# A retention and sparse-attention decoder: layer 1's y transposed by VectorE and carried through memory for three heads of four, and compression blocks made three ahead

## The chip, the cores and the metric

The program runs on one core of a Trainium2 chip. Its metric is the device time of one execution in microseconds. Five engines work side by side, each through its own queue in order: TensorE (PE, with its weight loads listed apart as PEld), VectorE (DVE), ScalarE (ACT), GpSimd (POOL) and SyncE (SP), which here only issues DMAs. The kernel before took 1155.59 us (median of three runs, 1155.13 to 1158.02).

## The reference, cut to what matters

Two layers over 512 tokens of width 1024, all float32. Layer 1 is a retention layer of four heads; for each head (256 wide in q and k, 512 in v):

```
q, k = rotary(x_norm @ Wq), rotary(x_norm @ Wk) / 16
o    = ((q k^T) * decay) @ v
o    = (o - mean(o)) * rsqrt(var(o) + eps)          # over the head's 512 columns
y    = silu(x_norm @ Wg) * o                        # 512 tokens x 512, per head
h   += (y * gain) @ Wout[512 h : 512 h + 512]       # 1024 columns
```

Between the layers, K and V of the sparse attention are projected once, and two of them are compressed: every block of 32 tokens (stride 16, 31 blocks, four groups) gets a position term, is flattened to 4096 numbers and goes through a small network:

```
blocks = (sub-blocks + pe).reshape(4, 31, 32 * 128)
k_cmp  = gelu(blocks @ w1) @ w2                      # w1: 4096 x 256; the same for v_cmp
```

Layer 2 is sparse attention over these, with a gate, an output projection and a per-layer embedding; the change does not touch it.

## The kernel before, in words

Every product of two float32 matrices is made of three matmuls (`mm3`, L349): each operand is held as a rounded high part and a low part, and high x high, high x low and low x high are summed in PSUM. ScalarE makes a high part (a copy that rounds), VectorE the low part (a subtraction of the high part).

Weights come as a stream of 176 blocks of 512 KB in the order in which they are used (`order`, L48; class `Stream`, L118). A block lands in one of four raw buffers (`load`, L143, on SP), is multiplied by its gain on POOL where it has one and is narrow (`mul`, L176), gets its high part from ScalarE (`high`, L190 or L194) and its low part from VectorE (`low`, L205 or L209), in one of six slots. After each `low` the next load goes into the raw buffer that came free. `W.tick()` does one `low`, one `high` and one `mul` of the blocks that are next; where a tick stands in the program decides where these stand in the engines' queues. The order of the program's lines is the order in each queue: there is no scheduler.

Layer 1 goes head by head (L546 to L582). For heads 1 to 3 it makes four projections of 128 columns (`proj_rot`, L409: q twice, k twice), each 24 matmuls of 512 columns, each followed by two multiplications by cosine and sine on VectorE (`rot_mul`, L423) and a tick; `rot_split` (L426) finishes the rotation on POOL and splits it on ScalarE and VectorE. Among these stands the transposition of the previous head's y: `retention_yT` (L516) for each of four token tiles, four 128 x 128 transposes on TensorE (L519) into PSUM and a split from there (L364, L365) into yH and yL. Then `out_proj` (L535) multiplies the previous head's y by its 512 rows of the output weights: eight tiles of 12 matmuls, each reading all four 128-column pieces of yH and yL of one token tile. The last head's y is transposed later, at L656, and keeps TensorE in both kernels.

The compression (`compress`, L779) runs twice, for K and for V, as eight steps of 12 matmuls of 256 columns (o at L797). Step s needs the block s: an addition on POOL (L787) into one of two buffers, a high part on ScalarE (L789), and a low part on VectorE (L792), in one of four pairs. Before the first step blocks 0 and 1 are made; step s then makes block s + 2. The second compression is spread among the four query projections of group 0 (`q_proj`, L732) at L867 to L877: two steps after each of the first three, and one on either side of the second half of the fourth. The first key projection (`k_proj`, L758) follows.

Of the kernel before, what the change touches and what calls it, by code (L numbers as in the profile page):

```python
# [11 lines left out]
F32 = mybir.dt.float32  # L12
F32R = mybir.dt.float32r
BF = mybir.dt.bfloat16
AF = mybir.ActivationFunctionType
# [3 lines left out]
NT, NK = 4, 8  # L19
# [217 lines left out]
def decoder(ctx: ExitStack, tc: tile.TileContext, x, xT, stream, cst, msk, gains, fnorm, out):  # L237
    nc = tc.nc
    pe, act, dve, pool = nc.tensor, nc.scalar, nc.vector, nc.gpsimd
    ctx.enter_context(tc.manual_schedule())  # L240
    sb = ctx.enter_context(tc.tile_pool(name="sb", bufs=1))
    ps = ctx.enter_context(tc.tile_pool(name="ps", bufs=1, space=bass.MemoryType.PSUM))
    nF = 4096 + 1024 * RAWS + 700 + 8192
    nR = 8192 + 2048 * SLOTS + 15104
# [4 lines left out]
    def V(o, n):  # L249
        assert o + n <= nF, (o, n)  # L250
        return arenaF[:, o:o + n]

    def R(o, n):
        assert o + n <= nR, (o, n)
        return arenaR[:, o:o + n]
# [8 lines left out]
    fb = 4096 + 1024 * RAWS  # L264
# [7 lines left out]
    def psum(tag, shape=None):  # L272
        n = {"d": 2, "s": 3, "pt": 2, "o": 1}[tag]
        return ps.tile([128, 512], F32, name=tag, bufs=n)
# [34 lines left out]
    yH = R(rb + 10752, 2048).rearrange("p (c n) -> p c n", c=4)  # L309
    yL = R(rb + 12800, 2048).rearrange("p (c n) -> p c n", c=4)  # L310
    gate = V(fb, 2048).rearrange("p (t n) -> p t n", t=NT)
# [2 lines left out]
    cs = V(fb + 4096, 1024).rearrange("p (a n) -> p a n", a=2)  # L314
    dec = V(fb + 5120, 1024).rearrange("p (h n) -> p h n", h=2)
    yb = [V(fb + 6144 + 512 * i, 512) for i in range(2)]
    rx = V(fb, 4096).rearrange("p (k t n) -> p k t n", k=NK, t=NT)


# [5 lines left out]
    o = psum("o")  # L325
    for i in range(30):
        pe.matmul(o[:, :256], masks[:, :128], masks[:, :256], start=True, stop=True)
    for k in range(NK):
        nc.sync.dma_start(rx[:, k], xT[k // 2, :, 512 * (k % 2):512 * (k % 2) + 512])
        if k in (0, 2):  # L330
            c = slice(256 * k, 256 * k + 512)
# [26 lines left out]
    def wst(p, o, k0=0, k1=NK):  # L358

        mm3(o, [(p.h[:, k], p.l[:, k], aH[:, :, k], aL[:, :, k]) for k in range(k0, k1)],  # L360
            k0 == 0, k1 == NK)
# [47 lines left out]
    def proj_rot(h, b, c):  # L409
        p = W.get("rin", 0, 1024, b + 256 * h + 128 * c, 128)  # L410
        o = psum("s" if h == 0 and b else "d")
        wst(p, o, 0, 4)
        if h or c == 0:
            W.tick()
        wst(p, o, 4, 8)
        p.done()
        if h == 0:
            return o
        rot_mul(o, c)

    def rot_mul(o, c):
        for i in range(2):
            dve.tensor_mul(rot[:, 2 * c + i], o, cs[:, i])  # L423
        W.tick()

    def rot_split(H, L):  # L426
        pool.tensor_sub(rot[:, 0], rot[:, 0], rot[:, 3])
        pool.tensor_add(rot[:, 1], rot[:, 1], rot[:, 2])
        for i in range(2):
            c = slice(512 * i, 512 * i + 512)  # L430
            act.activation(H[:, c], rot[:, i], AF.Copy)
            dve.tensor_sub(L[:, c], rot[:, i], H[:, c].bitcast(F32))
# [41 lines left out]
    def run(g):  # L474
        for _ in g:
            pass
# [39 lines left out]
    def retention_yT(t, bank="pt"):  # L516
        p = psum(bank)
        for c in range(4):
            pe.transpose(p[:, 128 * c:128 * c + 128], gate[:, t, 128 * c:128 * c + 128], ident)  # L519
        p3 = p.rearrange("p (c n) -> p c n", c=4)  # L520
        c = slice(128 * t, 128 * t + 128)
        split_psum(yH[:, :, c], yL[:, :, c], p3)

    def out_tile(t, c, p, YH, YL):
        o = psum("s" if t % 2 else "d")
        for a in range(2):
            mm3(o, [(YH[:, 2 * a + k, 128 * t:128 * t + 128], YL[:, 2 * a + k, 128 * t:128 * t + 128],
                     p[a].h[:, k], p[a].l[:, k]) for k in range(2)], a == 0, a == 1)
        d = hacc[:, t, 512 * c:512 * c + 512]
        dve.tensor_add(d, d, o)  # L530
# [15 lines left out]
    for h in range(HEADS):  # L546
        if h == 0:
            p = [W.get("rin", 0, 1024, 128 * c, 128) for c in (0, 1)]
            o = [psum("d") for c in (0, 1)]
            for k in range(NK):  # L550
                for c in (0, 1):
                    wst(p[c], o[c], k, k + 1)
                if k % 4 == 3:
                    W.tick()
            for c in (0, 1):
                p[c].done()
            dve.tensor_copy(masks, yb[0][:, :M_END])
            o += [proj_rot(h, 1024, c) for c in (0, 1)]
            rotary_scale()
            for b in range(2):  # L560
                for c in range(2):
                    rot_mul(o[2 * b + c], c)
                rot_split(*((kH, kL) if b else (qH, qL)))
        else:
            proj_rot(h, 0, 0)
            retention_yT(0)
            retention_yT(1)
            proj_rot(h, 0, 1)
            rot_split(qH, qL)
            retention_yT(2)  # L570
            retention_yT(3)
            proj_rot(h, 1024, 0)
            proj_rot(h, 1024, 1)
            rot_split(kH, kL)
            run(out_proj("rout", h - 1, yH, yL))
        tokens("rin", h, 2048, v_evac, ("o", "s", "pt", "pt") if h == 0 else ("d", "d", "s", "s"))
        retention_scores(h)
        if h < 3:
            load_decay(h + 1)
        tokens("rin", h, 4096, g_evac, ("d", "d", "pt", "pt"))  # L580
        for t in range(NT):
            retention_out(t)  # L582
# [74 lines left out]
    p = [out_pieces("rout", 3, c) for c in range(2)]  # L657
# [121 lines left out]
    def compress(b):  # L779

        def block(s):
            B = blk[s % 2].rearrange("p (l g n) -> p l g n", l=4, g=4)
            src = ckv[:, b]
            src = bass.AP(tensor=src.tensor, offset=src.offset + 4 * s,
                          ap=[list(src.ap[0]), [1, 4], [512, 4], [16, 31]])
            pos = gn[:, (G_PEV if b else G_PEK) + 4 * s:][:, :4]
            pool.tensor_add(B[:, :, :, :31], src,  # L787
                            pos[:, :, None, None].to_broadcast([128, 4, 4, 31]))
            act.activation(bkH[s % 4], blk[s % 2], AF.Copy)  # L789
            if s > 1:  # L790
                W.tick()
            dve.tensor_sub(bkL[s % 4], blk[s % 2], bkH[s % 4].bitcast(F32))  # L792

        block(0)
        block(1)
        yield
        o = psum("o")[:, :256]  # L797
        for s in range(8):
            p = W.get("wv" if b else "wk", 512 * s, 512, 0, 256)
            H, L = bkH[s % 4], bkL[s % 4]  # L800
            mm3(o, [(H[:, 128 * l:128 * l + 128], L[:, 128 * l:128 * l + 128], p.h[:, l], p.l[:, l])
                    for l in range(4)], s == 0, s == 7)
            if s < 6:
                block(s + 2)
            if s == 7:
                act.activation(hid, o, AF.Gelu_apprx_tanh)
            if s > 5:
                W.tick()
            p.done()
            yield  # L810
        tp = psum("pt")[:, :256]
        for c in range(2):
            pe.transpose(tp[:, 128 * c:128 * c + 128], hid[:, 128 * c:128 * c + 128], ident)
        if b == 0:
            split_psum(hidH.rearrange("p c n -> p (c n)"), hidL.rearrange("p c n -> p (c n)"), tp)
        else:
            src = tp.rearrange("p (a n) -> p a n", n=32)[:, :, None, :].to_broadcast([128, 8, 4, 32])
            split_psum(hrH.rearrange("p a (r n) -> p a r n", r=4),
                       hrL.rearrange("p a (r n) -> p a r n", r=4), src)
        yield  # L820
        w2 = [w[:, 2 * b:2 * b + 2] for w in (w2p.h, w2p.l)]
        if b == 0:
            o = psum("s")[:, :128]
            mm3(o, [(w2[0][:, c], w2[1][:, c], hidH[:, c], hidL[:, c]) for c in range(2)], True, True)
            split_psum(kcH, kcL, o)
        else:
            o = psum("s")
            for g in range(4):
                mm3(o[:, 128 * g:128 * g + 128],
                    [(hrH[:, 4 * c + g], hrL[:, 4 * c + g], w2[0][:, c], w2[1][:, c])  # L830
                     for c in range(2)], True, True)
            act.activation(vcat[:96], o[:96], AF.Copy)
            dve.tensor_sub(vcat[32:64], o[32:64], vcat[32:64].bitcast(F32))
        yield
# [6 lines left out]
    p = v_pieces(0)  # L841
    W.tick(1)
    o = [psum(bank)[:, :304] for bank in ("d", "o", "d", "s")]
# [190 lines left out]
    for g in range(GROUPS):  # L1034
        f = fillers(g)
        for u in range(8):
            h = u // 2
# [4 lines left out]
            n = PLAN[u] if g == 3 else left - first if u % 2 else first  # L1042
# [37 lines left out]
        if g < 3:  # L1080
            p = v_pieces(g + 1)
# [4 lines left out]
    p = [W.get("nout", 1792, 256, 512 * c, 512) for c in (0, 1)]  # L1086
# [98 lines left out]
```

## Time and profile before

| | |
|---|---|
| median of three runs | 1155.59 us |
| profiled execution: its own time | 1155.31 us |
| its span in the trace | 1153.3 us |
| TensorE busy | 1132.1 us, 98% |
| VectorE, ScalarE, GpSimd busy | 710.4, 486.7, 317.4 us |
| mean granted TensorE clock | 0.997 of full |
| moved by DMA | 101.9 MB, mean 88 GB/s |

The trace is one execution. A line of it names the line of the kernel, the engine, the operation, the tiles it writes and reads, and a count. A time in brackets in the timeline is how long the engine was idle before, and what ended that. Ends of matmuls are modelled: a matmul of 512 columns is listed at 0.39 us, while the next one starts 0.23 us after it. Nearly all tiles are parts of two large ones, arenaF (float32) and arenaR (the split parts), so the line tells more than the name.

### The profile page before, as it was taken

What the parts mean: (1) busy time and instruction counts of PE and PEld (TensorE: products, weight loads), DVE (VectorE), ACT (ScalarE), POOL (GpSimd) and SP (SyncE); (2) the same over time, 40 slices, a digit from 0 to 9 for tenths busy, and PEclk for the clock granted to TensorE, in tenths of its full rate; (3) what the DMA queues carried; (4) which work ended last, traced back from release to release, by engine and by line L of the source; (5) the groups of instructions that cost most, each with busy time, mean ns of one, the idle gap of its engine ahead of it and who ended that gap; (6) DMA issues with size and microseconds to landing.
All of it is one profiled execution on the core that took longest, in us unless ns stands there. A gap on an engine that the chain in (4) does not pass through costs nothing. (4 is left out here: it accounts for less than half of the span.)

```text
span 1153.3 us, 15259 instructions
## 1 busy us (share of the span) xinstructions
PE 1132.1 (98%) x5812; PEld 964.3 (84%) x5812; DVE 710.4 (62%) x1226; ACT 486.7 (42%) x916; POOL 317.4 (28%) x357
## 2 busy tenths in 40 slices
PE   9999999999999999999899999999999999999997
PEld 7888888888888888988777889888898888988886
DVE  4746435544634665656577865778468774788555
ACT  6433223223323454545455433444345443444653
POOL 0212003002200212346645332354153431421012
PEclk9999999999999999999999999999999999999999
DMA  8422331222232123244531211222031211221211
GB/s 329 149 97 73 110 101 55 92 101 74 86 116 73 55 78 106 73 152 160 163 110 56 74 37 39 78 85 66 27 93 55 74 56 44 85 85 44 74 37 73
DMA packets 29593, 101.90 MB, mean 88 GB/s; under 512 B 3536, under 2 KB 3792, under 8 KB 29520
## 3 DMA queue, kind: packets, MB, share of 16 engines
q1 hardware_dynamic: 29088, 100.15, 26.8%
q8 instruction: 45, 0.74, 0.3%
q10 hardware_dynamic: 432, 0.79, 0.2%
q14 instruction: 28, 0.23, 0.1%
HBM read 98.83 MB, written 2.10 MB: 88 GB/s over the span
## 5 line engine op out<-in xcount | busy, mean ns | idle before, releaser
L355 PE MATMUL d<-arenaR 128*128 128x512 f32 (+2 forms) x2904 | 676.5, 386 | 2.4 <-ACT arenaR L136 1.0
L355 PEld LDWEIGHTS d<-arenaR 128*128 128x128 f32 x2904 | 524.5, 188 | 103.2 <-DVE arenaF L753 1.4
L355 PE MATMUL s<-arenaR 128*128 128x512 f32 (+8 forms) x1182 | 239.8, 354 | 0.7 <-ACT arenaR L364 0.5
L205 DVE TENSOR_TENSOR arenaR<-arenaF,arenaR 128x1024 fp32r<-128x1024 f32 (+1 forms) x142 | 191.7, 1369 | 70.5 <-ACT arenaR L190 70.3
L355 PEld LDWEIGHTS s<-arenaR 128*128 128x128 f32 x1182 | 200.3, 188 | 30.6 <-ACT arenaR L364 0.7
L190 ACT ACTIVATE arenaR<-arenaF 128x1024 fp32r<-128x1024 f32 (+1 forms) x142 | 145.8, 1048 | 105.6 <-PE s L355 68.4
L176 POOL TENSOR_TENSOR arenaF<-arenaF 128x512 f32<-128x512 f32 x108 | 135.3, 1276 | 99.2 <-DMA arenaF<-stream_dram 94.7
L355 PE MATMUL o<-arenaR 128*128 128x512 f32 (+3 forms) x744 | 128.8, 322 | 6.3 <-DVE arenaR L792 4.1
L967 POOL TENSOR_SCALAR arenaF<-arenaF 128x512 f32<-128x512 f32 (+3 forms) x128 | 67.2, 545 | 232.3 <-ACT arenaR L364 118.8
L355 PEld LDWEIGHTS o<-arenaR 128*128 128x128 f32 x744 | 114.3, 189 | 19.6 <-DVE arenaR L792 5.1
L954 ACT ACTIVATE arenaF<-s,arenaF 128x512 f32<-128x512 f32 (+3 forms) x128 | 67.1, 526 | 101.4 <-DVE arenaF L947 90.6
L365 DVE TENSOR_TENSOR arenaR<-pt,arenaR 128x512 fp32r<-128x512 f32 (+1 forms) x141 | 82.9, 618 | 36.9 <-ACT arenaR L364 34.3
L364 ACT ACTIVATE arenaR<-pt 128x512 fp32r<-128x512 f32 (+1 forms) x141 | 70.8, 541 | 73.3 <-PE pt L976 35.2
L371 POOL TENSOR_TENSOR arenaF<-arenaF 128x1 f32<-128x1 f32 (+1 forms) x25 | 14.2, 570 | 295.3 <-DVE arenaF L370 295.3
L355 PE MATMUL pt<-arenaR 128*128 128x512 f32 (+1 forms) x384 | 75.9, 349 | 0.0
L355 PEld LDWEIGHTS pt<-arenaR 128*128 128x128 f32 x384 | 62.7, 188 | 9.4
L209 DVE SCALAR_TENSOR_TENSOR arenaR<-arenaF,arenaR 128x512 fp32r<-128x512 f32 x64 | 45.7, 763 | 35.1 <-PE pt L355 21.4
L194 ACT ACTIVATE arenaR<-arenaF 128x512 fp32r<-128x512 f32 x64 | 43.1, 720 | 46.7 <-issue 22.3
L947 DVE TENSOR_REDUCE arenaF<-s 128x1 f32<-128x512 f32 (+3 forms) x128 | 59.9, 489 | 3.3
L1015 DVE TENSOR_TENSOR arenaF<-arenaF,d 128x512 f32<-128x512 f32 x64 | 42.4, 683 | 8.6 <-PE d L355 7.8
L976 PEld LDWEIGHTS pt<-arenaF 128*128 128x128 f32 x318 | 38.3, 141 | 10.7 <-DVE arenaR L365 3.1
L976 PE MATMUL pt<-arenaF 128*128 128x128 f32 x318 | 45.1, 273 | 1.9 <-DVE arenaR L365 1.9
(126 smaller groups left out, 704.8 us busy)
## 6 DMA issues: line engine op xcount, KB each, us to landing
arenaF<-stream_dram SPq DMA_DIRECT2D x174, 512.0 KB, 3.6
arenaF<-xT_dram SPq DMA_DIRECT2D x8, 256.0 KB, 5.3
arenaF<-x_dram SPq DMA_DIRECT2D x4, 512.0 KB, 8.4
out_dram<-arenaF SPq DMA_DIRECT2D x3, 512.0 KB, 2.6
arenaF<-cst_dram SPq DMA_DIRECT2D x4, 256.0 KB, 3.9
arenaF<-stream_dram ACTq DMA_DIRECT2D x2, 256.0 KB, 4.2
arenaF<-stream_dram SPq DMA_DIRECT2D x2, 256.0 KB, 5.9
arenaF<-cst_dram SPq DMA_DIRECT2D x1, 512.0 KB, 9.5
```

The lines of the kernel that those rows point to most:

```text
L176: self.nc.gpsimd.tensor_mul(r3[:, k], r3[:, k], g[:, k, None].to_broadcast([128, m // 2, w]))
L190: self.nc.scalar.activation(hi[:, :m * w], raw, AF.Copy)
L194: self.nc.scalar.activation(hi[:, c], raw[:, c], AF.Copy, scale=g[:, k:k + 1])
L205: self.nc.vector.tensor_sub(lo[:, :m * w], raw, hi[:, :m * w])
L209: self.nc.vector.scalar_tensor_tensor(lo[:, c], raw[:, c], g[:, k:k + 1], hi[:, c], op0=OP.mult, op1=OP.subtract)
L355: pe.matmul(o, a, b, start=start and i == 0, stop=stop and i == n - 1)
L364: act.activation(h, src, AF.Copy)
L365: dve.tensor_sub(l, src, h.bitcast(F32))
L947: dve.reduce_max(mx[:, i:i + 1], o[:, f:f + 128 * i + 128], axis=mybir.AxisListType.X, negate=True)
L954: act.activation(Pu[:, PO[i]:PO[i] + n], o[:, f:f + n], AF.Exp, bias=mx[:, i:i + 1], accum_out=sm_[:, i:i + 1])
L967: pool.tensor_scalar(w, w, sm_[:, i:i + 1], 1.0, op0=OP.mult, op1=OP.mult)
L976: pe.transpose(p[:, f:f + 128], Pu[:, PO[i] + 128 * j:PO[i] + 128 * j + 128], ident)
```

## The change

For heads 1 to 3 TensorE no longer transposes the previous head's y. VectorE transposes each 32 x 32 block of it in place (`retention_blocks`: two instructions for two token tiles, into a free stretch of arenaF, yt). Four DMAs write yt to a buffer in device memory, one for each of its four groups of 32 partitions, so that the blocks come to stand in transposed order; one DMA brings the buffer back over the y it came from (`retention_back`). `retention_split` then makes yH and yL from SBUF where the split before read PSUM. The four splits stand after the last of the four projections, in front of `rot_split` of k.

In the compression three blocks are made ahead in place of two, and step s makes block s + 3; the ticks keep their number and their steps. The two buffers of the addition and the four pairs stay.

```diff
+    dr = ctx.enter_context(tc.tile_pool(name="dr", bufs=2, space=bass.MemoryType.DRAM))
+    yt = V(fb + 7168, 1024)
+    def view(a, o, *ap):
+        return bass.AP(tensor=a.tensor, offset=a.offset + o, ap=[list(a.ap[0])] + [list(d) for d in ap])
+    moved = [None, None]
+    def retention_blocks(i):
+        for t in range(2):
+            dve.transpose(view(yt, 128 * t, (32, 4), (256, 4), (1, 32)),
+                          view(gate, 512 * (2 * i + t), (128, 4), (32, 4), (1, 32)))
+        m = moved[i] = dr.tile([128, 1024], F32, name="moved")
+        for a in range(4):
+            nc.sync.dma_start(bass.AP(tensor=m.tensor, offset=m.offset + 256 * a,
+                                      ap=[[1024, 32], [32 * 1024, 4], [1, 256]]),
+                              yt[32 * a:32 * a + 32].rearrange("p (b n) -> p b n", b=4))
+    def retention_back(i):
+        nc.sync.dma_start(gate[:, 2 * i:2 * i + 2].rearrange("p t n -> p (t n)"), moved[i])
+    def retention_split(t):
+        src = view(gate, 1024 * (t // 2) + 128 * (t % 2), (32, 4), (256, 4), (1, 32))
+        c = slice(128 * t, 128 * t + 128)
+        h, l = (y[:, :, c].rearrange("p c (a n) -> p c a n", a=4) for y in (yH, yL))
+        act.activation(h, src, AF.Copy)
+        dve.tensor_sub(l, src, h.bitcast(F32))
...
             proj_rot(h, 0, 0)
-            retention_yT(0)
-            retention_yT(1)
+            retention_blocks(0)
             proj_rot(h, 0, 1)
+            retention_back(0)
             rot_split(qH, qL)
-            retention_yT(2)
-            retention_yT(3)
+            retention_blocks(1)
             proj_rot(h, 1024, 0)
+            retention_back(1)
             proj_rot(h, 1024, 1)
+            for t in range(NT):
+                retention_split(t)
             rot_split(kH, kL)
...
-            if s > 1:
+            if s > 2:
                 W.tick()
...
         block(0)
         block(1)
+        block(2)
...
-            if s < 6:
-                block(s + 2)
+            if s < 5:
+                block(s + 3)
...
-            if s > 5:
+            if s > 4:
                 W.tick()
```

VectorE's queue from head 1's first projection to its first output tile stood before as follows (L423 rot_mul, L209 and L205 low parts of weights, L365 the split of y from PSUM, L432 the split of q or k, L530 the output tile's addition).

```order
L423 TENSOR_TENSOR arenaF<-d,arenaF 128x512 x2
L209 SCALAR_TENSOR_TENSOR arenaR<-arenaF,arenaR 128x512 x2
L365 TENSOR_TENSOR arenaR<-pt,arenaR 128x4x128 x2
L209 SCALAR_TENSOR_TENSOR arenaR<-arenaF,arenaR 128x512 x2
L423 TENSOR_TENSOR arenaF<-d,arenaF 128x512 x2
L432 TENSOR_TENSOR arenaR<-arenaF,arenaR 128x512 x2
L365 TENSOR_TENSOR arenaR<-pt,arenaR 128x4x128 x2
L209 SCALAR_TENSOR_TENSOR arenaR<-arenaF,arenaR 128x512 x2
L423 TENSOR_TENSOR arenaF<-d,arenaF 128x512 x2
L205 TENSOR_TENSOR arenaR<-arenaF,arenaR 128x1024
L423 TENSOR_TENSOR arenaF<-d,arenaF 128x512 x2
L432 TENSOR_TENSOR arenaR<-arenaF,arenaR 128x512 x2
```

In the changed kernel the same stretch reads, from the first transposition on (L536 the transposes, L425 rot_mul, L434 the split of q or k, L552 the split of y):

```order
L536 STREAM_TRANSPOSE arenaF<-arenaF 128x4x4x32 x2
L209 SCALAR_TENSOR_TENSOR arenaR<-arenaF,arenaR 128x512 x2
L425 TENSOR_TENSOR arenaF<-d,arenaF 128x512 x2
L434 TENSOR_TENSOR arenaR<-arenaF,arenaR 128x512 x2
L536 STREAM_TRANSPOSE arenaF<-arenaF 128x4x4x32 x2
L209 SCALAR_TENSOR_TENSOR arenaR<-arenaF,arenaR 128x512 x2
L425 TENSOR_TENSOR arenaF<-d,arenaF 128x512 x2
L205 TENSOR_TENSOR arenaR<-arenaF,arenaR 128x1024
L425 TENSOR_TENSOR arenaF<-d,arenaF 128x512 x2
L552 TENSOR_TENSOR arenaR<-arenaF,arenaR 128x4x128 x4
L434 TENSOR_TENSOR arenaR<-arenaF,arenaR 128x512 x2
```

The transposes took the places of the splits, and the four splits stand together behind the last rot_mul.

SP's queue for head 1 in the changed kernel holds ten more DMAs (L143 the weight stream, L540 the writes to memory, L545 the way back):

```order
L143 DMA arenaF<-stream_dram 128x1024 x5
L540 DMA moved<-arenaF 32x4x256 x4
L143 DMA arenaF<-stream_dram 128x1024
L545 DMA arenaF<-moved 128x1024
L540 DMA moved<-arenaF 32x4x256 x4
L143 DMA arenaF<-stream_dram 128x1024
L545 DMA arenaF<-moved 128x1024
L143 DMA arenaF<-stream_dram 128x1024 x9
```

Before, these sixteen loads of the stream stood in one row.

VectorE's queue at the start of the second compression stood before as follows (L792 the blocks' low parts, L365 and L740 splits of the hidden values and of a query, L205 low parts of weights):

```order
L205 TENSOR_TENSOR arenaR<-arenaF,arenaR 128x1024 x3
L792 TENSOR_TENSOR arenaR<-arenaF,arenaR 128x512 x2
L365 TENSOR_TENSOR arenaR<-pt,arenaR 128x256
L740 SCALAR_TENSOR_TENSOR arenaR<-d,arenaR 128x512
L205 TENSOR_TENSOR arenaR<-arenaF,arenaR 128x1024 x2
L792 TENSOR_TENSOR arenaR<-arenaF,arenaR 128x512
```

In the changed kernel (L824 the blocks, L367 and L772 the splits):

```order
L205 TENSOR_TENSOR arenaR<-arenaF,arenaR 128x1024 x3
L824 TENSOR_TENSOR arenaR<-arenaF,arenaR 128x512 x3
L367 TENSOR_TENSOR arenaR<-pt,arenaR 128x256
L772 SCALAR_TENSOR_TENSOR arenaR<-d,arenaR 128x512
L205 TENSOR_TENSOR arenaR<-arenaF,arenaR 128x1024 x2
L824 TENSOR_TENSOR arenaR<-arenaF,arenaR 128x512
```

A third block stands ahead of the splits and of the low part of the next weights.

## Rows read from the trace of the kernel before

**Rows 1.** Page, part 1: busy us, share of the span, instructions, by engine.
```profile
PE 1132.1 (98%) x5812; PEld 964.3 (84%) x5812; DVE 710.4 (62%) x1226; ACT 486.7 (42%) x916; POOL 317.4 (28%) x357
```

**Rows 2.** Waits of PE: us in total, times, longest.
```profile
PE o L355 <- DVE arenaR L792: 4.1, 5, 1.6
```

**Rows 3.** Timeline of PE, 88 to 93: start, us, instructions, count.
```profile
90.41 1.03 PE L519 MATMUL pt<-arenaF 128*128 128x128 f32 x8
91.20 2.07 PE L355 MATMUL d<-arenaR 128*128 128x512 f32 x8
```

**Rows 4.** Timeline, 101 to 117: head 1, up to its output projection.
```profile
100.30 1.09 DVE L432 TENSOR_TENSOR arenaR<-arenaF,arenaR 128x512 fp32r<-128x512 f32 x1 [2.06 <-ACT arenaR L431]
100.82 10.59 PE L355 MATMUL d<-arenaR 128*128 128x512 f32 x46
...
102.15 1.28 DVE L365 TENSOR_TENSOR arenaR<-pt,arenaR 128x512 fp32r<-128x512 f32 x2
...
105.87 1.22 DVE L205 TENSOR_TENSOR arenaR<-arenaF,arenaR 128x1024 fp32r<-128x1024 f32 x1
108.50 1.06 ACT L190 ACTIVATE arenaR<-arenaF 128x1024 fp32r<-128x1024 f32 x1 [4.38 <-PE d L355]
108.72 1.29 DVE L423 TENSOR_TENSOR arenaF<-d,arenaF 128x512 f32<-128x512 f32 x2 [1.64 <-PE d L355]
110.09 1.29 POOL L427 TENSOR_TENSOR arenaF<-arenaF 128x512 f32<-128x512 f32 x1 [9.25 <-DVE arenaF L423]
```

**Rows 5.** Page, part 6: DMA issues, count, KB each, us to landing.
```profile
arenaF<-stream_dram SPq DMA_DIRECT2D x174, 512.0 KB, 3.6
...
out_dram<-arenaF SPq DMA_DIRECT2D x3, 512.0 KB, 2.6
```

**Rows 6.** Timeline, 540 to 552: the second compression's first steps.
```profile
540.59 2.56 POOL L787 TENSOR_TENSOR arenaF<-arenaF 128x496 f32<-128x496 f32 x2
...
542.59 1.95 DVE L792 TENSOR_TENSOR arenaR<-arenaF,arenaR 128x512 fp32r<-128x512 f32 x2 [3.87 <-ACT arenaR L789]
...
544.46 0.42 DVE L365 TENSOR_TENSOR arenaR<-pt,arenaR 128x256 fp32r<-128x256 f32 x1
...
544.79 0.68 DVE L740 SCALAR_TENSOR_TENSOR arenaR<-d,arenaR 128x512 fp32r<-128x512 f32 x1
545.39 3.19 DVE L205 TENSOR_TENSOR arenaR<-arenaF,arenaR 128x1024 fp32r<-128x1024 f32 x2
...
546.49 2.91 PE L355 MATMUL d<-arenaR 128*128 128x512 f32 x12
```

**Rows 7.** Timeline, 552 to 582: its later steps and the key projection.
```profile
554.72 1.46 PE L355 MATMUL o<-arenaR 128*128 128x256 f32 x10 [0.21 <-DVE arenaR L792]
...
556.37 2.13 POOL L176 TENSOR_TENSOR arenaF<-arenaF 128x512 f32<-128x512 f32 x2 [5.39 <-DMA arenaF<-stream_dram]
...
559.78 0.63 ACT L789 ACTIVATE arenaR<-arenaF 128x512 fp32r<-128x512 f32 x1 [5.36 <-POOL arenaF L787]
...
563.27 2.89 PE L355 MATMUL o<-arenaR 128*128 128x256 f32 x22 [1.39 <-DVE arenaR L792]
...
570.52 0.50 PE L355 MATMUL o<-arenaR 128*128 128x256 f32 x2 [1.61 <-ACT arenaR L789]
...
571.41 1.56 PE L355 MATMUL o<-arenaR 128*128 128x256 f32 x10 [0.38 <-DVE arenaR L792]
...
572.77 4.43 PE L355 MATMUL d<-arenaR 128*128 128x512 f32 x12
...
577.47 1.52 DVE L792 TENSOR_TENSOR arenaR<-arenaF,arenaR 128x512 fp32r<-128x512 f32 x1
...
579.05 1.46 PE L355 MATMUL o<-arenaR 128*128 128x256 f32 x10 [1.61 <-DVE arenaR L792]
...
580.35 2.00 PE L355 MATMUL d<-arenaR 128*128 128x512 f32 x8
```

**Rows 8.** Windows: us, busy time by engine, granted clock, DMA share, GB/s.
```profile
572.70:577.00 4.30, 4.30 (x14) 3.44 (x13) 1.52 (x2) 2.50 (x3) 3.81 (x4) 0.61 0.35 122
```

## The prediction

> **What bounds the kernel now.** I read the page first: TensorE is busy for 98% of the span [rows 1], so a microsecond counts only where TensorE loses it, to work that goes or to a wait. Then the list of TensorE's waits. Its largest row is the second compression: matmuls into o wait for the blocks' low parts from VectorE, 4.1 us in five waits [rows 2]. Then the timeline of the two places that the change touches: head 1 of layer 1 [rows 3, 4] and the second compression [rows 6, 7]. Last, the granted clock behind the compression's waits [rows 8].
>
> The change has two parts on two places of the path. The first takes work from TensorE and puts a wait on it; the second takes waits away and adds one.
>
> **Part 1, what goes.** Per head two groups of eight transposes. The first stands at 90.41, where the next matmul would have started, and the last of the following eight matmuls starts at 91.20 + 2.07 - 0.39 = 92.88. Matmuls in a row start every (10.59 - 0.39) / 45 = 0.227 us [rows 4], so without the group it would start at 90.41 + 7 x 0.227 = 92.00 [rows 3]. A group costs 0.88 us, six groups 5.3 us. The splits from PSUM go too, but VectorE and ScalarE get as many from SBUF; TensorE waited for none of them.
>
> The Trainium skill ("VectorE: DVE Perf Modes", section "The three transpose paths") gives 390 ns for a 128 x 128 transpose on TensorE and 311 ns for its 32 x 32 blocks on VectorE, both in bf16. By the first, an estimate, 48 transposes would give back 18.7 us; the trace shows 0.11 us each in a row of eight, and the trace decides.
>
> **Part 1, what comes.** Before, yH and yL of the old head were ready long before the output projection, and it followed the last projection without a gap: of the run of 46 matmuls the last 12 are its first tile, which starts at 100.82 + 34 x 0.227 = 108.53 [rows 4]. Call this moment 0. Now the four splits stand behind the last projection in both queues. ScalarE first has the tick's L190, which needs the weight slot that this projection frees: it ran from -0.03, 1.06 us [rows 4]. Then the first split, 0.63 us by the copy of the same size [rows 7]: yH is there at 1.6 to 1.7, and the first two matmuls run. The third reads yL. VectorE has the two multiplications from 0.19, 1.29 us, then the subtraction, from about 1.65. It takes 0.64 us by the splits of y before; beside POOL, which starts rot_split as VectorE ends the multiplications (110.09, 0.08 us after 110.01), it takes 1.09 us by L432 [rows 4]. So yL is there at 2.3 to 2.75 and the third matmul starts then, not at 0.45: 1.9 to 2.3 us lost. POOL will be there, so I take 2.2 us, three times: 6.6 us. Part 1 by itself is +1.3 us.
>
> What the other added steps cost, and what hides it:
> - The transposes, four per head, on VectorE. None is in the trace. Above zero a faster one gives nothing, since TensorE doesn't wait there. The splits whose places they take cost 0.64 each; the dearest instruction of 128 x 512 in these rows took 1.52 [rows 7]. I take 0.68, the nearest in shape and place. The cover is VectorE's idle time before the last multiplications, 1.64 us [rows 4], less the 0.88 by which TensorE's second saved group outruns VectorE (the first moves both): about 0.75 us, plus 0.1 at the subtraction. What exceeds 0.85 us per head is paid.
> - The way through memory. Tiles 2 and 3 are the later ones: their transposes end near 102.5 (the splits in their place at 103.43, less 0.88) [rows 4], the writes land 2.6 to 3.6 us after their issue, the way back 3.6 us later [rows 5], some issuing between: near 110 to 111. TensorE, 1.76 us ahead of before, wants tile 2 after 24 matmuls, at 106.8 + 2.2 + 5.4 = 114.4. Cost nothing; if over 3 us late, paid in full. ScalarE and VectorE stand behind the third split until then, and behind them rot_split of k and the output tiles' additions, which TensorE wants later still.
> - SP's queue waits at each way back until its four writes have landed, and the next load behind it is late by that. Its weights get their low parts only in or after the output projection: nothing.
>
> **Part 2, what goes.** From 546.49 (first half of the second query projection) to 580.35 (key projection) TensorE takes 33.86 us. In it are five waits, 0.21, 1.39, 1.61, 0.38 and 1.61 us [rows 6, 7]. A matmul's modelled end hides some 0.15 us more of each, together 0.8. And the half projection at 572.77 took 4.43 us against 2.91 for the same twelve matmuls at 546.49 [rows 6, 7]; its window shows a granted clock of 0.61 [rows 8], so the clock stood at 1.2 GHz for most of it, right after the two waits before. That is 1.5 us. Work without all this: 33.86 - 5.2 - 0.8 - 1.5 = 26.3 us. The waits have one cause: POOL adds the next block only behind the gain of the next weights, which waits 5.39 us for its DMA, and ScalarE then waits 5.36 for POOL [rows 7]. One step earlier in the queue, blocks 4 and 6 come before such a gain, and blocks 5 and 7 get a step's and a half projection's time more. Of the five waits of rows 2 (4.1 us) four are among these, the fifth wait here being ScalarE's; the one left, 0.5 us for the first block, stays.
>
> **Part 2, what comes.** The third block made ahead stands before the low part of the second query's weights. POOL can add it only when block 0's subtraction has freed the buffer (542.59 + 1.1 = 543.7); addition 1.28 to 545.0, ScalarE 0.63 to 545.7, VectorE 0.68 to 1.1 to 546.4 or 546.8. Then L365, L740 and the low part, 0.42 + 0.68 + 1.22 to 1.6: 548.7 to 549.5 [rows 4, 6, 7]. Before, that low part was ready as the projection began. Its third matmul, 0.45 us after 546.49, waits 1.8 to 2.6 us; I take 2.2. Part 2 gives 33.86 - 26.3 - 2.2 = 5.3 us, if the weights keep up: the last block's low part and the last step's weights then come within half a microsecond of their use, so up to 1 us of it may be lost again.
>
> **The clock.** The change sets four new waits of about 2.2 us where TensorE ran through. In the trace the clock fell after 1.61 and 0.38 us close together, not after 1.39 or 1.61 alone [rows 7, 8]. The new ones are longer than any of these. I charge one fall in four, 1.5 us. The Trainium skill ("TensorE: Matmul & The Clock Gate", section "Part 1: The HAM clock gate") says that the clock is halved by how busy the engine has lately been; the trace agrees (0.61).
>
> **Sum.** Against the profiled execution's 1155.3 us (span 1153.3 and 2.0 around it; the median of the runs is 1155.6): 1155.3 + 1.3 - 5.3 + 1.5 = 1152.8 us. No fall of the clock gives 1151.3, all four 1157.3.
>
> **Rivals.**
> - *The new waits don't show.* The subtractions run undisturbed (1.9 per head, part 1 at +0.4), the third block's delay is hidden (part 2 at -7.5) and the clock holds: 1155.3 + 0.4 - 7.5 = 1148.2 us. For it: VectorE's subtractions vary by 0.4 us with what POOL does beside them [rows 4], and the clock held after single waits. Against it: the queues are in order, and both places have a named instruction that ends late. Half of this gives 1150.5.
> - *VectorE becomes the bound ahead of the output projection.* If a transpose costs 1.52 us, four cost 3.4 us more than the splits they replace, less 0.85 of cover: 2.5 us a head, three heads 7.5: 1160.3 us. It ends slower than before from 1.4 us each. For it: an instruction form that the trace doesn't show, with a scattered output. Against: as many elements as its neighbours. The skill's 311 ns, four times for 128 x 512, would be an estimate of 1.24 us each and a sum near 1157; no run here shows it yet.
> - *The compression gives little.* The waits move from the blocks to the weights behind the same DMA, POOL and ScalarE: with 2 us gained in place of 5.3, 1156.1 us. For it: the half microsecond of room at the last step. Against: four of the five waits have the block, not the weights, as the last to come.
>
> **How the numbers follow.** Forecast 0.56, new waits that don't show 0.16, VectorE as the bound 0.15, little from the compression 0.13. The forecast's own range is 1150.3 to 1156.5, by the bounds of the waits and the falls. A difference of 0.3% (3.5 us) is what a measurement can tell here: faster means below 1152.1, slower above 1159.1. Faster: the first rival and a third of the forecast, 0.35. Slower: the second rival and a little of the forecast's end, 0.16. Within: 0.49. The range 1149.0 to 1160.0 leaves out part of the first two rivals.
>
> **What would show it.** In the changed profile: no transposes of y on TensorE for the first three heads; at each of three output projections a wait of 1.5 to 2 us for ScalarE's L551 and a second of 0.3 to 0.8 for VectorE's L552; transposes of 0.6 to 0.8 us; in the second compression one wait of about 2 us for L205 in the query projection, no wait for blocks but the first, and no clock below 1 there. It is wrong if the transposes take over 1 us, if L551 waits for a DMA while TensorE stands, or if the steps of the compression wait for weights.

## The result and the profile after

The changed kernel takes 1164.5 us (median of 4 runs, 1163.9 to 1164.9), the kernel before 1155.4 (4 runs, 1154.5 to 1158.0). The ratio is 1.0082, with a 95% interval of 1.0068 to 1.0097: slower by 9.2 us. I had predicted 1152.8 us and a range up to 1160.0, so the sign and the range were both wrong. The profiled execution took 1164.2 us with a span of 1162.4, 9.1 us longer than before.

The page's first part, against [rows 1]: the 48 transposes are gone from TensorE (5764 instructions in place of 5812), and yet it is busy for longer.

```profile
PE 1134.2 (98%) x5764; PEld 963.5 (83%) x5764; DVE 724.2 (62%) x1238; ACT 486.7 (42%) x916; POOL 318.1 (27%) x357
```

The list of TensorE's waits (us in total, times, longest), against [rows 2]:

```profile
PE d L357 <- ACT arenaR L551: 4.3, 3, 1.4
PE d L357 <- DVE arenaR L552: 3.3, 3, 1.1
PE s L357 <- ACT arenaR L366: 2.4, 1, 2.4
...
PE d L357 <- DVE arenaR L205: 1.8, 2, 1.6
PE s L357 <- DVE arenaR L367: 1.1, 1, 1.1
...
PE o L357 <- DVE arenaR L205: 0.9, 1, 0.9
...
PE o L357 <- DVE arenaR L824: 0.8, 2, 0.6
```

The blocks' waits fell from 4.1 us to 0.8 (L824 is L792 of before). The first two rows and L205's in front of d are waits that the prediction had named. L205's in front of o, 0.9 us, is the compression's last step waiting for its weights: one of the prediction's signs of being wrong, for which it had allowed up to 1 us. L366 with L367, the split of the second compression's key, is one that it had not.

Head 1's output projection in the timeline (start, us, engine, line, count, idle before and what ended it), against [rows 4]:

```profile
105.75 1.06 ACT L190 ACTIVATE arenaR<-arenaF 128x1024 fp32r<-128x1024 f32 x1 [4.37 <-PE d L357]
105.97 1.29 DVE L425 TENSOR_TENSOR arenaF<-d,arenaF 128x512 f32<-128x512 f32 x2 [0.59 <-PE d L357]
...
106.71 1.13 ACT L551 ACTIVATE arenaR<-arenaF 128x512 fp32r<-128x512 f32 x2
107.34 1.28 POOL L429 TENSOR_TENSOR arenaF<-arenaF 128x512 f32<-128x512 f32 x1 [8.34 <-DVE arenaF L425]
107.36 1.81 DVE L552 TENSOR_TENSOR arenaR<-arenaF,arenaR 128x512 fp32r<-128x512 f32 x1
...
107.38 0.73 PE L357 MATMUL d<-arenaR 128*128 128x512 f32 x2 [1.44 <-ACT arenaR L551]
108.58 1.73 POOL L430 TENSOR_TENSOR arenaF<-arenaF 128x512 f32<-128x512 f32 x1
...
109.23 4.06 PE L357 MATMUL d<-arenaR 128*128 128x512 f32 x10 [1.11 <-DVE arenaR L552]
110.16 1.15 ACT L551 ACTIVATE arenaR<-arenaF 128x512 fp32r<-128x512 f32 x2 [2.31 <-DMA arenaF<-moved]
```

Two things are larger than forecast. The subtraction L552 takes 1.81 us: POOL's L429 started 0.02 us ahead of it. And the ten matmuls behind the second wait take 4.06 us, 0.41 each, against 0.227 in a full row. The windows of this stretch and of the one behind the key projection show the reason in the granted clock (behind the busy times; then DMA share and GB/s):

```profile
109.00:112.50 3.50, 3.27 (x8) 2.60 (x9) 3.50 (x5) 2.19 (x4) 1.30 (x1) 0.51 0.33 136
...
557.00:575.00 18.00, 17.83 (x103) 15.51 (x104) 13.21 (x14) 9.36 (x13) 7.77 (x6) 1.00 0.54 177
...
593.70:600.60 6.90, 6.57 (x20) 5.80 (x21) 5.16 (x14) 2.89 (x9) 2.88 (x5) 0.51 0.16 64
```

TensorE stood at its lower level, 1.2 GHz. The same windows at 211 and 313.5 us, the other two heads, show 0.57 and 0.55. Inside the compression the clock is now full.

The second compression, against [rows 6, 7]:

```profile
554.64 0.63 PE L357 MATMUL d<-arenaR 128*128 128x512 f32 x2
...
556.86 2.60 PE L357 MATMUL d<-arenaR 128*128 128x512 f32 x10 [1.59 <-DVE arenaR L205]
...
583.91 5.86 PE L357 MATMUL d<-arenaR 128*128 128x512 f32 x24
...
586.02 8.25 POOL L176 TENSOR_TENSOR arenaF<-arenaF 128x512 f32<-128x512 f32 x6 [0.69 <-DMA arenaF<-stream_dram]
...
589.32 1.06 ACT L190 ACTIVATE arenaR<-arenaF 128x1024 fp32r<-128x1024 f32 x1 [2.63 <-POOL arenaF L176]
...
590.39 1.28 ACT L911 ACT_TABLE_LOAD   x1
...
591.79 0.58 ACT L366 ACTIVATE arenaR<-d 128x512 fp32r<-128x512 f32 x1
...
592.43 0.49 PE L357 MATMUL s<-arenaR 128*128 128x512 f32 x1 [2.44 <-ACT arenaR L366]
...
594.03 4.26 PE L357 MATMUL s<-arenaR 128*128 128x512 f32 x14 [1.11 <-DVE arenaR L367]
...
598.09 4.28 PE L357 MATMUL d<-arenaR 128*128 128x512 f32 x13
```

The same place in the kernel before, behind its key projection:

```profile
586.67 0.50 PE L355 MATMUL s<-arenaR 128*128 128x512 f32 x1 [0.47 <-ACT arenaR L364]
587.39 2.38 PE L355 MATMUL s<-arenaR 128*128 128x512 f32 x14 [0.22 <-DVE arenaR L365]
589.61 5.63 PE L355 MATMUL d<-arenaR 128*128 128x512 f32 x24
```

From the second query projection to the key projection it now takes 583.91 - 554.64 = 29.27 us, 4.6 less than the 33.86 of before: nearly the forecast 5.3. The key projection stands 3.56 us behind its place of before, and the end of the span 9.1: so another 5.5 us are lost behind it. ScalarE's key split L366 is queued behind L190, which waits for POOL's gain L176, and behind an ACT_TABLE_LOAD (L911, 1.28 us) that stands between the two and is held back too. TensorE waits 2.44 and 1.11 us where it waited 0.47 and 0.22, and then runs mostly at 1.2 GHz for 6.9 us.

### The profile page after: what moved, and what is told of

It reads as the page before. It is cut to its first block, busy times and chain, and to the rows that moved or that the text cites. A ratio compares the mean times of both kernels' runs of the same rounds, so it can differ in the third digit from the quotient of the medians.

```text
span 1162.4 us, 15225 instructions
## 1 busy us (share of the span) xinstructions
PE 1134.2 (98%) x5764; PEld 963.5 (83%) x5764; DVE 724.2 (62%) x1238; ACT 486.7 (42%) x916; POOL 318.1 (27%) x357
## 5 line engine op out<-in xcount | busy, mean ns | idle before, releaser
L205 DVE TENSOR_TENSOR arenaR<-arenaF,arenaR 128x1024 fp32r<-128x1024 f32 (+1 forms) x142 | 190.8, 1363 | 66.8 <-ACT arenaR L190 66.4
L190 ACT ACTIVATE arenaR<-arenaF 128x1024 fp32r<-128x1024 f32 (+1 forms) x142 | 145.6, 1048 | 118.8 <-PE s L357 76.0
L176 POOL TENSOR_TENSOR arenaF<-arenaF 128x512 f32<-128x512 f32 x108 | 137.0, 1291 | 98.3 <-DMA arenaF<-stream_dram 98.1
L367 DVE TENSOR_TENSOR arenaR<-pt,arenaR 128x512 fp32r<-128x512 f32 (+1 forms) x129 | 75.1, 611 | 35.5 <-ACT arenaR L366 33.1
L366 ACT ACTIVATE arenaR<-pt 128x512 fp32r<-128x512 f32 (+1 forms) x129 | 64.3, 536 | 73.4 <-PE pt L1009 35.2
L209 DVE SCALAR_TENSOR_TENSOR arenaR<-arenaF,arenaR 128x512 fp32r<-128x512 f32 x64 | 45.5, 759 | 35.0 <-PE pt L357 21.4
```

The lines of the kernel that those rows point to most:

```text
L176: self.nc.gpsimd.tensor_mul(r3[:, k], r3[:, k], g[:, k, None].to_broadcast([128, m // 2, w]))
L190: self.nc.scalar.activation(hi[:, :m * w], raw, AF.Copy)
L205: self.nc.vector.tensor_sub(lo[:, :m * w], raw, hi[:, :m * w])
L209: self.nc.vector.scalar_tensor_tensor(lo[:, c], raw[:, c], g[:, k:k + 1], hi[:, c], op0=OP.mult, op1=OP.subtract)
L366: act.activation(h, src, AF.Copy)
L367: dve.tensor_sub(l, src, h.bitcast(F32))
```

## The experiments

Each was timed beside the kernel before on the same chip; ratios are to it (1155.2, 1154.9 and 1155.2 us in the three sets).

**e1_layer1_only.** Part 1 alone; the compression as before.

```diff
-            if s > 2:
+            if s > 1:
                 W.tick()
...
-        block(2)
...
-            if s < 5:
-                block(s + 3)
+            if s < 6:
+                block(s + 2)
...
-            if s > 4:
+            if s > 5:
                 W.tick()
```

> Layer 1 as changed, the compression as before. Theory (waits): at each of three output projections TensorE loses 2.9 us to the splits that now stand behind the last projection and 1.5 us to the clock that falls after it, and gains 1.8 us of transposes: +2.7 us a head, +8 us, 1163.5 us. Rival (the parts are entangled: part of the compression's loss comes from the state in which layer 1 leaves the weight stream): +5 to +6 us.

1163.4 us, 1.0070 [1.0058, 1.0082]: +8.2. The waits are those of the changed kernel to 0.01 us, and in all three heads the clock falls behind them (0.61 to 0.62 in the windows). Part 1 makes nearly all of the loss.

**e2_compress_only.** Part 2 alone, in the kernel before.

```diff
-            if s > 1:
+            if s > 2:
                 W.tick()
...
+        block(2)
...
-            if s < 6:
-                block(s + 2)
+            if s < 5:
+                block(s + 3)
...
-            if s > 5:
+            if s > 4:
                 W.tick()
```

> Three blocks ahead, layer 1 as before. Theory: 4 us gained up to the key projection and all of it given back behind it, where the split of the keys stands on ScalarE behind the high part of weights that wait for their gain: 0 to +2 us, 1155.5 to 1157.5, and the trace shows a wait of about 2.4 us for that split. Rival (the loss came with layer 1): the wait does not appear, -4 us, 1151.5.

1156.5 us, 1.0011 [1.0003, 1.0020]: +1.2. The compression is shortened, and TensorE then waits 2.44 us for the key's split and 0.68 and 0.72 more; the clock stands at 0.56 for the 7.5 us behind. All that part 2 gains is given back there. The two parts add up: 8.2 + 1.2 = 9.4, against 9.2 together.

**e4_fill.** e1 with eight matmuls, whose result nothing reads, in the place of the first wait: it leaves the queues and the second wait as they are, and keeps TensorE at work.

```diff
             proj_rot(h, 1024, 1)
+            z = psum("pt")
+            for i in range(8):
+                pe.matmul(z, qH[:, :128], qH[:, 512:1024], start=True, stop=True)
```

> Layer 1 as changed, plus eight matmuls of 512 columns into an unused bank behind the last projection of heads 1 to 3, whose result nobody reads; compression as before. They take 1.8 us of time in which TensorE waits anyway. Theory (a third of each head's loss is the clock): no half-clock stretch behind them, 1.5 us less per head than layer 1 alone, 4.5 us in all, 1159 us. Rival (the clock is not what costs, or busy matmuls don't hold it): as layer 1 alone or above, 1163 to 1165.

1157.9 us, 1.0023 [1.0014, 1.0032]: 5.4 us less than e1, by work that is thrown away. Matched matmul by matmul, 4.4 us of the two profiled executions' difference lie in layer 1; the rest came later, mostly in the first key projection, which e1's execution ran partly at the lower clock (24 matmuls in 7.08 us, here 5.63). The second wait is still there, and behind it:

```profile
106.20 1.98 PE L606 MATMUL pt<-arenaR 128*128 128x512 f32 x8
...
109.65 2.57 PE L357 MATMUL d<-arenaR 128*128 128x512 f32 x10 [1.01 <-DVE arenaR L552]
```

The same ten matmuls take 2.57 us in place of 4.06: 1.5 us a head are the clock's. The window over this stretch has a granted clock of 1.00, in the two other heads too.

**e5_rot_late.** e1 with POOL's half of k's rotation behind the first output tile in the program, to free the subtraction from POOL.

```diff
+            f = out_proj("rout", h - 1, yH, yL)
+            next(f)
             rot_split(kH, kL)
-            run(out_proj("rout", h - 1, yH, yL))
+            run(f)
```

> Layer 1 as changed, but the rotation's end of k (two POOL additions and its split) stands behind the first output tile; compression as before. Theory (the low part of y takes 1.8 us because POOL adds beside it): without POOL it takes 0.7 us, TensorE's second wait goes from 1.1 to 0.1 us, 3.3 us less than layer 1 alone (1160), and if the shorter idle time no longer drops the clock 4.5 us less again (1155.5). Rival (the low part is slow by its strided form): the subtraction stays near 1.8 us, 1163.

1162.1 us, 1.0069 [1.0057, 1.0082]. It says nothing of POOL: POOL's queue holds no instruction of the output tile, so L429 still began at the same moment (107.72, 0.01 us ahead of L552), and both waits stayed. It does tell of the clock. In head 2 and head 3, after the same 1.44 and 1.11 us:

```profile
213.26 2.56 PE L357 MATMUL d<-arenaR 128*128 128x512 f32 x10 [1.11 <-DVE arenaR L552]
...
314.05 3.98 PE L357 MATMUL d<-arenaR 128*128 128x512 f32 x10 [1.11 <-DVE arenaR L552]
```

It held once and fell once (and fell in head 1). Over the changed kernel, e1 and this run, the clock fell behind these two waits in 8 of 9 heads. What spared the ninth is open.

**e12_pool_later.** e1 with the second multiplication of k's last half behind the first two splits. POOL needs its result, so POOL now really starts later.

```diff
...
-            proj_rot(h, 1024, 1)
-            for t in range(NT):
+            o = proj_rot(h, 1024, 1, raw=True)
+            dve.tensor_mul(rot[:, 2], o, cs[:, 0])
+            W.tick()
+            for t in range(2):
+                retention_split(t)
+            dve.tensor_mul(rot[:, 3], o, cs[:, 1])
+            for t in range(2, NT):
```

> Layer 1 as changed, but the last of the two multiplications of k's last projection stands behind the first two splits on VectorE, so that POOL cannot add beside them; compression as before. Theory (POOL slows the low part of y): the first subtraction takes 0.7 us, not 1.8, TensorE's second wait falls from 1.1 to about 0.2 us, 3 us less than layer 1 alone (1160), 4.5 us less again where the clock then holds (1155.5). Rival (the strided form is slow): 1.8 us stays, 1163.

1156.3 us, 1.0008 [0.9999, 1.0017]: 7.0 less than e1. The timeline of head 1:

```profile
107.63 1.29 DVE L552 TENSOR_TENSOR arenaR<-arenaF,arenaR 128x512 fp32r<-128x512 f32 x2 [0.69 <-ACT arenaR L551]
107.65 3.28 PE L357 MATMUL d<-arenaR 128*128 128x512 f32 x12 [1.44 <-ACT arenaR L551]
...
109.61 1.29 POOL L429 TENSOR_TENSOR arenaF<-arenaF 128x512 f32<-128x512 f32 x1 [10.33 <-DVE arenaF L608]
...
110.86 1.30 POOL L430 TENSOR_TENSOR arenaF<-arenaF 128x512 f32<-128x512 f32 x1
...
111.34 1.36 DVE L552 TENSOR_TENSOR arenaR<-arenaF,arenaR 128x512 fp32r<-128x512 f32 x1 [1.82 <-ACT arenaR L551]
```

The two first subtractions take 1.29 us together, the second wait is gone, and the twelve matmuls run at the full clock behind the first wait of 1.44 us, in all three heads. The last row shows the price again: this subtraction began inside POOL's L430, which ended at 112.16, and ended 0.54 us later.

**e3_split_early.** e1 with tiles 0 and 1 split one projection earlier.

```diff
+            for t in range(2):
+                retention_split(t)
             proj_rot(h, 1024, 1)
-            for t in range(NT):
+            for t in range(2, NT):
```

> Layer 1 as changed, but the first two splits stand before the last projection; compression as before. Theory (waits): TensorE runs into the output projection without a wait, except up to 0.8 us at the third tile, the clock holds, and the saved transposes show: -5.3 + 0 to 2.5, 1150.2 to 1152.7 us. Rival (the transposes on VectorE and the way through memory cost the time, wherever the splits stand): stays above 1157.

1153.0 us, 0.9981 [0.9972, 0.9991]: 10.4 less than e1. No wait is left in heads 1 and 3, and the clock holds. In head 2 the other half is late: the third split waits for the way back from memory.

```profile
210.56 1.15 ACT L551 ACTIVATE arenaR<-arenaF 128x512 fp32r<-128x512 f32 x2 [5.44 <-DMA arenaF<-moved]
...
211.25 3.06 PE L357 MATMUL d<-arenaR 128*128 128x512 f32 x11 [1.55 <-ACT arenaR L551]
```

**e10_l1_earlier.** e3 with the second pair of transposes ahead of q's rotation too.

```diff
+            retention_blocks(1)
             rot_split(qH, qL)
-            retention_blocks(1)
```

> Layer 1 with the first two splits before the last projection and the second pair of transposes before the rotation's end of q; compression as before. Theory (what was left in the early splits was the way back from memory, 1.7 us at one third tile): the way back is issued about 2 us sooner, no wait in the three heads, 1155 - 5.3 + 0 to 1, 1149.7 to 1151 us. Rival (the memory way is late by its own time, not by when it starts): as with the early splits alone, 1153.

1149.4 us, 0.9952 [0.9939, 0.9965]: 5.9 less than before. No wait of these splits is left. The 5.3 us of the transposes are there to be had; the changed kernel lost them by where it put the splits.

**e6_third_at_step0.** e2 with the third block one step later, to take away the query projection's wait.

```diff
-        block(2)
...
+            if s == 0:
+                block(2)
```

> Compression alone (layer 1 as before), with two blocks ahead of the first step and two made at step 0, so three ahead from there. Theory (the third block ahead of the first step delays the second query's low part): the wait of 1.6 us in that projection goes, 1.7 us less than the compression alone, 1154.8. Rival (the weight stream sets the last step whatever comes before): the last step waits that much longer, no change, 1156.5.

1156.2 us, 1.0011 [1.0001, 1.0020], as e2. The query projection's wait went from 1.59 to 0.14 us, new ones of 0.88, 0.22 and 0.41 came later in the compression, and the key's split waits 2.44 us as before.

**e7_tick_after_key.** e2 with the weights' tick of the last step behind the key's split in ScalarE's queue.

```diff
-            if s > 4:
+            if s > 4 and not (b and s == 7):
                 W.tick()
...
+    W.tick(1)
```

> Compression alone as changed, with the second compression's last tick moved behind the first key projection. Theory (the split of the keys is late because it stands behind the high part of weights that wait for their gain): the waits behind the key projection shrink from 4.4 to about 1.1 us and the clock holds there (3.4 us), 6 us less than the compression alone, 1150.5. Rival (the weights then come late for a later projection, or the clock falls elsewhere): 1154 to 1156.

1155.1 us, 0.9998 [0.9988, 1.0007], 1.4 less than e2. The key's split is back at waits of 0.47 and 0.22 us, which shows that ScalarE's order made the long one. But the next in the chain is POOL: its two small casts of the key wait beside VectorE's low parts.

```profile
584.05 2.54 DVE L205 TENSOR_TENSOR arenaR<-arenaF,arenaR 128x1024 fp32r<-128x1024 f32 x2
...
584.31 1.20 POOL L764 CAST arenaR<-arenaR 128x32 fp32r<-128x32 f32 x1
585.45 1.20 POOL L765 CAST arenaR<-arenaR 128x32 fp32r<-128x32 f32 x1
...
585.56 0.46 PE L355 MATMUL s<-arenaR 128*128 128x416 f32 x1 [0.64 <-POOL arenaR L764]
```

The clock fell there all the same (0.57 in the 8 us from 585).

**e11_c_both.** The edits of e6 and e7 together, layer 1 as before. Against e2:

```diff
-        block(2)
...
+            if s == 0:
+                block(2)
...
-            if s > 4:
+            if s > 4 and not (b and s == 7):
...
+    W.tick(1)
```

> Compression alone, third block at step 0 and last tick behind the key projection, layer 1 as before. Theory (the two changes of queue order need each other: each alone leaves the other's wait and the clock's fall): -4 to -5 us, 1150 to 1151.5. Rival (the gain of the kernel with both parts mended came from layer 1): 1154 to 1156.

1155.0 us, 0.9996 [0.9988, 1.0005]: nothing gained. Matched matmul by matmul, the compression is 4.0 us shorter, and 4.7 are lost behind it. The waits ahead are small, but POOL's gain waits 2.03 us for its weights' DMA, the cast is queued behind it, and TensorE waits 2.63 us for the cast.

**e9_both_earlier.** The edits of e10, e6 and e7 together. Against the changed kernel:

```diff
+            retention_blocks(1)
             rot_split(qH, qL)
-            retention_blocks(1)
...
+            for t in range(2):
+                retention_split(t)
             proj_rot(h, 1024, 1)
-            for t in range(NT):
+            for t in range(2, NT):
                 retention_split(t)
...
-        block(2)
...
+            if s == 0:
+                block(2)
...
-            if s > 4:
+            if s > 4 and not (b and s == 7):
...
+    W.tick(1)
```

> Both parts with their waits taken away: first two splits before the last projection, the second pair of transposes before the rotation's end of q, third block at step 0, last tick behind the key projection. Theory: 5.3 us of transposes and 6 to 8 us of the compression come out together, 1142 to 1145 us. Rival (the memory way or the weight stream gives part back): 1147 to 1151.

1145.8 us (1144.8 to 1148.5), 0.9925 [0.9912, 0.9937]: faster than both kernels, by 9.1 and 18.7 us. Its list of waits, where no split of y and no block over 0.2 us is left:

```profile
PE o L357 <- DVE arenaR L205: 2.2, 3, 0.9
...
PE s L357 <- ACT arenaR L366: 0.5, 1, 0.5
PE d L357 <- DVE arenaR L205: 0.4, 1, 0.4
PE o L357 <- DVE arenaR L826: 0.4, 2, 0.2
```

Here the gain's data came 0.17 us after POOL was free, and the casts ran ahead of the low parts, in 0.21 us each. So part 2 is worth some 3.3 us beside this layer 1 (9.1 against e10's 5.9 less than before) and nothing beside the old one (e11).

What differs between the two is one load. In both, the block of weights that POOL's gain waits for is issued 0.57 us after the key projection's first matmul; it lands 3.9 us after its issue here and 5.7 in e11. While it is under way in e11, a packet of an instruction queue stands among the DMA traffic (575.7 to 581.5: packets, MB, share of 16 engines):

```profile
q8 instruction: 1, 0.02, 1.4%
```

Here no packet of that queue falls into the stretch (570.6 to 574.6). The other traces with a shortened compression go the same way: e2, e6 and e7, with layer 1 as before, have one at this place and take 5.2, 5.2 and 4.7 us for the load; the changed kernel has none and takes 3.8. That this packet delays the load is an inference: no run moves it alone.

## Why the prediction was wrong

The prediction was 11.7 us too low (1152.8 against 1164.5). Four of its terms make this up.

*The subtraction beside POOL (2.1 us).* Step "beside POOL ... it takes 1.09 us by L432", 2.2 us per head. The two waits took 1.6 and 1.28 us with the matmul's modelled end, 2.9. The subtraction ran 1.81 us. I had the right row and read it as a slower rate. It is a wait: L432 of [rows 4] began inside POOL's second addition and ended 0.54 us after it. Three rows agree, each counted from the end of POOL's instruction:

| subtraction | POOL's ends | it ends | later by | its time |
|---|---|---|---|---|
| before, L432 at 100.30 | 100.85 | 101.39 | 0.54 | 1.09 |
| after, L552 at 107.36 | 108.62 | 109.17 | 0.55 | 1.81 |
| e12, L552 at 111.34 | 112.16 | 112.70 | 0.54 | 1.36 |

So the price is what is left of POOL's instruction, plus 0.54 us; I had written that POOL starts just ahead of the subtraction, and by this reading all of POOL's 1.28 us stand ahead of it. The Trainium skill says so ("SBUF — State Buffer", section "SBUF: two separate sides"): a VectorE instruction with two SBUF inputs and a POOL instruction that reads SBUF need the same pair of ports, the one that starts first holds it for its whole instruction, and the other stands. The trace agrees by these three rows, and in which forms suffer. Two groups by shape of the changed kernel with an input from PSUM (pt, d; count, then busy us and mean ns):

```profile
L367 DVE TENSOR_TENSOR arenaR<-pt,arenaR 128x512 fp32r<-128x512 f32 x90 | 57.9, 685 | 16.5 <-ACT arenaR L366 14.1
...
L425 DVE TENSOR_TENSOR arenaF<-d,arenaF 128x512 f32<-128x512 f32 x28 | 18.0, 684 | 4.2 <-PE d L357 4.2
```

And its twelve subtractions L552 (lowest, median, highest ns):

```profile
L552 DVE TENSOR_TENSOR arenaR<-arenaF,arenaR x12: 678/1224/1815, 107.4 to 316.0; 128x512 fp32r<-128x512 f32 x12
```

With an input from PSUM the mean is 685 ns. Of L552, with both from SBUF, the first two of each head ran beside POOL and took 1.76 to 1.82 us; the last two had no POOL instruction beside them and took 0.68 to 0.69. So it is not the strided form that costs. The change had replaced L367 by L552, a split from PSUM by one from SBUF, and I had called the two equal ("VectorE and ScalarE get as many from SBUF"). e12 shows it for the first subtraction: with POOL later, 0.69 us.

*The clock in layer 1 (3.0 us).* "I charge one fall in four, 1.5 us." The size of a fall was right (4.06 - 2.57 = 1.5). It fell in all three heads, and held behind the fourth new wait, the query projection's 1.59 us. The case "all four 1157.3" was in the text, with too small a weight. The prediction's own rows pointed the other way: the fall that it had seen came behind two waits close together, and it had forecast two close together in each head. e12 bears this out: with the first wait alone, 1.44 us, the clock held in all three. e4 shows the clock's share apart from the waits' (1.5 us a head).

*What stands behind the compression (6.0 us).* Part 2's sum ended at the key projection. There its step was nearly right: 4.6 us gained of 5.3. But ScalarE's queue holds the next weights' high part ahead of the key's split, and those weights had not come closer. TensorE arrived earlier and waited 2.44 + 1.11 us in place of the 0.47 + 0.22 of before, to which e7 returns without this order: 2.9 more. Behind it 14 matmuls took 4.26 us against 2.38 before, and the next 13 took 4.28 against some 3.05 (13 / 24 of before's 5.63): 3.1 more at half the clock. The prediction put this at nothing without a reason. (Matched matmul by matmul, 6.1 us are lost within 21 us of the key projection's start; by the end of the span it is 5.5, since 0.5 comes back in layer 2.) The rival "the compression gives little" had the mechanism (weights behind the same DMA, POOL and ScalarE) and too mild a price.

*The gain itself (0.7 us)*: 4.6 in place of 5.3. The last step's wait for its weights, 0.94 us, is the loss of up to 1 us that the prediction had named and left out of the sum. Together 2.1 + 3.0 + 6.0 + 0.7 = 11.8.

Right were these. The first wait per head was 1.44 us (1.5 to 2 forecast; 1.6 with the matmul's modelled end), the query projection's 1.59 (about 2), and the blocks' waits went but for 0.8 us. The transposes were cheap, as the rows of L536 (ns, lowest, median, highest) show, so VectorE never became the bound:

```profile
L536 DVE STREAM_TRANSPOSE arenaF<-arenaF x12: 701/708/712, 92.2 to 305.7; 128x512 f32<-128x512 f32 x12
```

The 5.3 us that TensorE gains from them are borne out by e10 (5.9). The way through memory was in time in the changed kernel: no wait of L551 there goes back to it. In e3, where TensorE comes earlier, it was 1.55 us late in one head of three, which I had priced at nothing.

## What to carry to other kernels

Before a split is moved from PSUM to SBUF inputs, look at what POOL does in the same microsecond: the price is the rest of POOL's instruction, and a consumer that is next on TensorE pays it. Where a stage is sped up, follow the sum past its end to the next instruction that waits for a load, since a queue in order hands the gain to whatever stands there. Where two new stalls stand close together on a full TensorE, count them twice, once as the waits and once as the matmuls behind them at the lower clock; behind single stalls of 1.4 to 1.6 us the clock held here (e12, e3, e2). And first try to move the producer one step earlier: that alone turned +8.2 us into -5.9.

## What the runs showed of the hardware

- POOL pays too. Its addition L430 took 1.73 us when it came up inside a VectorE subtraction (1.29 and 1.30 in e12, where it started first), and a cast of 32 columns 1.20 us beside VectorE's low parts (0.21 ahead of them).
- Eight matmuls whose result is thrown away made the kernel 5.4 us faster (e4): in all three heads the clock then held through a wait of 1.0 us, which is 4.4 us of it.
- Equal waits need not have equal results: after 1.44 and 1.11 us the clock fell in 8 heads and held in one.
- The transposes of 32 x 32 blocks took 0.70 to 0.71 us for 128 x 512, with a scattered output. No POOL instruction stood beside any of the twelve, so these runs don't say what one would do.
